# A macaron layer on one core: the scan's states, gates and squares get scheduling priority, and eight modulation sums move into the second feed-forward sublayer

## The chip, the cores and the metric

The kernel runs on one core of a Trainium2 chip. The metric is the device time of one execution in microseconds (us), as the median of several runs; less is better. A core has a matrix engine (PE, with the loading of its weights shown apart as PEld), a vector engine (DVE), a scalar engine (ACT), GpSimd (POOL) and an engine SP whose queue issues the transfers from memory (DMA). Each takes its instructions in a fixed order, and semaphores make one wait for another.

## What is computed

One layer on 512 tokens of width 1024: feed-forward 1, a mixer, feed-forward 2, each behind a norm whose shift, scale and gate come from a vector `c`, and a last norm. Cut from the reference:

```python
mod = silu(c) @ w_ada + b_ada        # 9 vectors of 1024: shift, scale, gate of 3 sublayers
x = x + 0.5 * gate0 * swiglu(modulate(rmsnorm(x), shift0, scale0), ffn1_in, ffn1_out)
x = x +       gate1 * hybrid_mixer(modulate(rmsnorm(x), shift1, scale1), ...)
x = x + 0.5 * gate2 * swiglu(modulate(rmsnorm(x), shift2, scale2), ffn2_in, ffn2_out)
x = rmsnorm(x, final_g)

def swiglu(h, w_in, w_out):
    a, b = jnp.split(h @ w_in, 2, axis=-1)
    return (jax.nn.silu(a) * b) @ w_out

def hybrid_mixer(h, ...):            # 24 heads of 64 in 4 groups
    u_pool, z, xbc, dt_raw = split(h @ w_in)
    y_pool = pool_mixer(u_pool, w_pool, pool_scale)   # windowed means, 4 windows
    xs, Bm, Cm = split(silu(causal_depthwise_conv(xbc)))
    y = ssd_chunked(xs, softplus(dt_raw), A, Bm, Cm) + d_skip * xs
    y = y * silu(z)
    y = y * lax.rsqrt(mean(y * y over the group) + EPS) * ssm_norm_g
    return concatenate([y_pool, y]) @ w_out
```

## The kernel before

**Matrix work.** Activations lie as 128 features by 512 tokens. Each fp32 product is made of three reduced-precision matmuls (L376 to L378) from a high and a low part of both sides. Weights come as raw blocks of 128x1024 (tile `w_raw`, three buffers); ACT casts the high part (L168), DVE subtracts to get the low part (L171), and both go into rings `w_hi` and `w_lo` of five. PE's order is written out by hand and fixed. The order on DVE, ACT, POOL and SP is made by a scheduler, which follows the program's order, dependences and priorities; `tc.high_priority()` raises the instructions inside it, and `keep_in_program_order` holds one to its place among others so marked.

**The mixer** goes through 46 tiles of products, n = 0 to 45: 33 of the in-projection (their order stands in a list), 8 called outA (n = 33 to 40) and 5 called outB. Tile n = 33 begins about 628 us into the execution. Between products the scan runs for 12 pairs of heads. Pair p has five steps at written times: `fetch`, `one` (transposes L1032, then exponentials L1037 on ACT and two products L1048 on DVE), `two` (PE states L1061 and diagonal part L1065, which reads L1048's result; then four states L1074 and the skip L1077 on DVE), `three` (PE L1087, which reads L1074's result; the gate: DVE L1088, POOL L473 and L1090) and `squares` (ACT L528, or L525 for a group's first pair, then POOL L473). Three pairs are a group: its squares are summed on PE (L494), a chain of ten small DVE operations takes the root (L507, L479, L481 to L488), PE spreads it over the partitions (L517), and DVE and ACT scale and split the group's outputs (L1108, L467, L469). The windowed means run on ACT, POOL and PE (L872 to L890), and outA adds to x by L603.

**Modulation sums.** Each of the 72 columns of `mod` is one DVE operation over 128x1024 (L549, with a read of the accumulator behind it), fed by a 512 KB transfer into a `w_raw` buffer (L559). A generator yields after each sum, `pump(n)` asks it for n, and it always loads one row ahead:

```python
for j, k in steps[len(ws):i + 2]:
    ws.append(self.W.block())
    self.nc.sync.dma_start(out=ws[-1], in_=self.a["ada"][j, k])
ins = self.ada_sum(*step, ws[i])
```

Before, the mixer makes the 32 sums of vectors 5, 7, 6 and 8: one at n = 1 to 8, at each even n from 10 to 32, one at each of the last four outA tiles, two in each outB tile. Vector 8 is the gate of feed-forward 2.

**Feed-forward 2.** After two halves of the norm come three plain pairs (`pair`, gated product L686), then 17 `quad`s that save matmuls by sums of halves. `combine` prepares these in four pumped steps of DVE and ACT work (L396, L400, L469). In a quad, DVE L440 adds PE's block y to `one`, and PE's block z, in the other half of y's bank, starts only when L440 has read y:

```python
block(y, ws[n:], [(act, HALF_A) for act in up], True)
V.tensor_tensor(out=one[:, la], in0=one[:, la], in1=y, op=ALU.add)   # L440
...
block(x, ws[n:], t2, False)
block(z, ws[:n], t1, True)
```

Feed-forward 1 is built alike, with sums of other vectors pumped between its quads.

Of the kernel before, what the change touches and what calls it, by code (L numbers as in the profile page):

```python
# [1 line left out]

# [1 line left out]

# [8 lines left out]
ALU = mybir.AluOpType  # L13
PSUM = bass.MemoryType.PSUM

P = 128
# [14 lines left out]
LATE2 = 2  # L31
MLATE = 5
SPREAD1, SPREAD2, SPREAD3 = 3.6, 1.8, 2.4
# [28 lines left out]
FULL = (0, NT)  # L62
# [220 lines left out]
class Block:  # L283
# [136 lines left out]
    def quad(self, h, g, outs):  # L420
# [39 lines left out]
        for src, c in ((two, lb), (x, la)):  # L460
            V.scalar_tensor_tensor(out=two[:, c], in0=src[:, c], scalar=-1.0, in1=one[:, c], op0=ALU.mult, op1=ALU.mult)
        self.split(two, *g)

    def split(self, src, hi, lo, sl=FULL, pool=False):
# [521 lines left out]
    @staticmethod  # L986
    def c_(c):
        return slice(c * P, (c + 1) * P)
# [64 lines left out]
    def two(self, p):  # L1053

        V, S, T, c_, v4 = self.nc.vector, self.nc.scalar, self.nc.tensor, self.c_, self.v4
        st = self.pair_st[p]
        heads, xd, xe, xs = st["heads"], st["xd"], st["xe"], st["xs"]
        btok = self.grp[p // 3]["btok"]
        pst = self.bank("t")
        for c in range(3):  # L1060
            T.matmul(pst[:, c_(c)], lhsT=btok[:, c_(c)], rhs=xe[:, c_(c)], start=True, stop=True)  # L1061
        yd = self.bank("y")
        for c in range(NCHK):
            for r in range(2):
                T.matmul(yd[64 * r:64 * (r + 1), c_(c)], lhsT=xd[:, c * P + 64 * r:c * P + 64 * (r + 1)],  # L1065
                         rhs=st["e"][r][:, c_(c)], start=True, stop=True)
        s = st["s"] = self.tmp()
        S.copy(out=s[:, c_(0)], in_=pst[:, c_(0)])
        ec = st["ec"]
        S.activation(out=ec[:, :3 * P], in_=ec[:, :3 * P], func=AF.Exp)  # L1070
        for c in (1, 2):
            for r in range(2):
                o = c * P + 64 * r
                V.scalar_tensor_tensor(out=s[:, o:o + 64], in0=s[:, o - P:o - P + 64],  # L1074
                                       scalar=self.dec[:, c, 2 * p + r:2 * p + r + 1], in1=pst[:, o:o + 64],
                                       op0=ALU.mult, op1=ALU.add)
        V.scalar_tensor_tensor(out=xs, in0=xs, scalar=self.vec[:, C_DS + p:C_DS + p + 1], in1=yd,  # L1077
                               op0=ALU.mult, op1=ALU.add)

    def three(self, p):  # L1080

        V, S, T, G, c_ = self.nc.vector, self.nc.scalar, self.nc.tensor, self.nc.gpsimd, self.c_
        st, gr = self.pair_st.pop(p), self.grp[p // 3]
        y, ec = st["xs"], st["ec"]
        yo = self.bank("y")
        for c in range(3):
            T.matmul(yo[:, c_(c)], lhsT=st["s"][:, c_(c)], rhs=gr["ct"][:, c_(c + 1)], start=True, stop=True)  # L1087
        V.tensor_tensor(out=ec[:, :3 * P], in0=ec[:, :3 * P], in1=yo[:, :3 * P], op=ALU.mult)  # L1088
        self.accumulate(y[:, P:], ec[:, :3 * P])
        G.tensor_tensor(out=y, in0=y, in1=self.z.pop(p), op=ALU.mult)  # L1090
        gr["y"].append(y)

    def squares(self, p):
        gr = self.grp[p // 3]
        if p % 3 == 0:
            gr["acc"] = self.big()
        self.square_into(gr["y"][p % 3], FULL, gr["acc"], p % 3 == 0)

    def group_sums(self, g):
        gr = self.grp[g]  # L1100
# [12 lines left out]
    def mixer(self, norm, after):  # L1113
        V = self.nc.vector
        self.z, self.convd, self.grp, self.pair_st = {}, {}, {}, {}
        acts = self.acts = {}
        h = norm.h
        order = self.mixer_order()
        self.cwh = self.vec[:, C_CW:C_CW + 100]
        self.sgh = self.vec[:, C_SG:C_SG + 12]  # L1120
        for t in (self.cwh, self.sgh):
            self.tc.keep_in_program_order(V.tensor_scalar(out=t, in0=t, scalar1=0.5, scalar2=None, op0=ALU.mult))

        def z_halves(pss, sl):
            for i, ps in enumerate(pss):
                self.silu_z(i, ps, sl)

        self.wdt = self.big()
        self.nc.sync.dma_start(out=self.wdt[:, :KD * 32], in_=self.a["w_dt"])
        self.in_halves(4, norm, z_halves)  # L1130
        self.bg = self.ada_steps((5, 7, 6, 8), True)
        plan = []

        def at(time, f, *args):
            plan.append((time, f, args))
            plan.sort(key=lambda e: e[0])

        def until(time):
            while plan and plan[0][0] <= time:
                _, f, args = plan.pop(0)  # L1140
                f(*args)

        for p, s in enumerate(STARTS):
            g = p // 3
            if p % 3 == 0:
                at(s + HEAD, self.head, g)
            for d, f in zip(STAGES, (self.fetch, self.one, self.two, self.three, self.squares)):
                at(s + d, f, p)
            if p % 3 == 2:
                at(s + SUMS, self.group_sums, g)  # L1150
                at(s + NORM, self.group_norm, g)

        self.wpool = None

        def pool(i, ps):
            if self.wpool is None:
                self.wpool = self.big()
                self.nc.sync.dma_start(out=self.wpool, in_=self.a["w_pool"])
            d = self.pool_mix(i, ps)

            def later():
                acts[i] = self.new_act()
                self.pool_out(i, d, acts[i])

            at(POOLS[i], later)

        def conv(i, ps):
            self.convd[i] = self.conv(i, ps)

        for n, (kind, i) in enumerate(order):  # L1170
            until(n)
            self.pump({"outA": i // 4, "outB": 2}.get(kind, 0 < n < 9 or n > 9 and n % 2 == 0))
            if kind in ("dt", "in"):
                ps = self.bank()
                if kind == "dt":
                    for part in range(2):
                        for k in range(KD):
                            o = 32 * (k % 4)
                            self.nc.tensor.matmul(ps[o:o + 32, :], lhsT=self.wdt[:, k * 32:(k + 1) * 32],
                                                  rhs=h[k][part].bitcast(F32), start=part == 0 and k < 4,  # L1180
                                                  stop=part == 1 and k >= 4)
                    dt = self.dt_all(ps)
                    for d in DT:
                        at(n + d, next, dt, None)
                    continue
                self.product(ps, None, h, mid=lambda f: until(n + f))
                if i < 4:
                    at(n + EVAC, pool, i, ps)
                elif i < 16:
                    at(n + EVAC, self.silu_z, i - 4, ps, FULL)  # L1190
                else:
                    at(n + EVAC, conv, i - 16, ps)
            else:
                ks = range(4, 10) if kind == "outA" else LAST_KS
                at(n + 1, self.out_full(i, [acts[k] for k in ks], 5, kind == "outB", lambda f: until(n + f)))
        until(len(order))
        assert not plan
        self.out_halves(range(MLATE, KD), [acts[k] for k in ks], 5, after(), SPREAD2)

    def run(self):  # L1200
        h, gs = self.start()
        norms = {}

        def norm(sub):
            norms[sub] = Norm(self, sub)
            return norms[sub]

        self.ffn(1, h, gs, 2, lambda: norm(1), LATE1, SPREAD1, (1, 1))
        self.mixer(norms[1], lambda: norm(2))
        gs = {j: self.new_act() for j in range(FIRST[2])}  # L1210

        def glu_halves(pss, sl):
            for i in range(2):
                self.glu(pss[2 * i], pss[2 * i + 1], sl, gs[i])

        self.in_halves(4, norms[2], glu_halves)
        final = Final(self, 0)
        self.bg = self.combine(norms[2].h)
        self.ffn(2, norms[2].h, gs, 8, lambda: final, LATE2, SPREAD3, (2, 0))
        final.finish()  # L1220


# [81 lines left out]
```

## Time and profile before

| | |
|---|---|
| median of 3 runs (lowest to highest) | 1098.95 us (1098.39 to 1099.58) |
| the profiled execution | 1098.18 us |
| its span, first to last instruction | 1096.3 us |
| granted TensorE clock, mean | 0.998 |
| PE / PEld busy | 1075.5 / 954.4 us |
| DVE / ACT / POOL busy | 851.2 / 500.6 / 116.9 us |

Busy time is the time in which an engine had an instruction running; the span is that of the profiled execution, with 1.9 us outside it. Matmuls overlap, so a busy PE is only one that had no gap. The feed-forwards and the mixer follow one another: feed-forward 2 is under way at 750 us and ends at the span's end.

### The profile page before, as it was taken

To read this page: it belongs to the slowest core of one execution; us is meant where nothing else is said; L and a number is where in the kernel's file an instruction comes from. 1 tells how busy PE (TensorE), PEld (TensorE's weight loads), DVE (VectorE), ACT (ScalarE), POOL (GpSimd) and SP (SyncE) were. 2 spreads that over 40 slices of the span, in tenths; PEclk is the share of its full clock that TensorE was granted. 3 is DMA by queue.
4 is the path that set the end of the run, shared out by engine and by line. 5 is a ranking of instruction groups with operands and counts; after the bars stand their busy time and mean duration, and the time that the engine had idled before them with its cause. 6 is when DMAs were issued, how large, how long until landed. Compare 5 with 4: busy or idle time off the path is not lost.

```text
span 1096.3 us, 17024 instructions
## 1 busy us (share of the span) xinstructions
PE 1075.5 (98%) x6764; PEld 954.4 (87%) x6764; DVE 851.2 (78%) x1354; ACT 500.6 (46%) x836; POOL 116.9 (11%) x114
## 2 busy tenths in 40 slices
PE   8999999999999999999999999999999999999997
PEld 7888899999899988887888767899899999999997
DVE  7986978888887848989988777764877778777744
ACT  4442444454444544656565552354434434444532
POOL 0000000000001410012312850121000000000011
PEclk9999999999999999999999999999999999999999
DMA  8865334443346405554445335740132233223222
GB/s 326 305 225 175 127 120 135 144 144 126 111 158 204 152 25 167 173 168 138 144 135 182 122 120 173 231 153 20 42 113 86 91 113 107 95 87 101 75 58 78
DMA packets 45955, 149.43 MB, mean 136 GB/s; under 512 B 5276, under 2 KB 8220, under 8 KB 45876
## 3 DMA queue, kind: packets, MB, share of 16 engines
q1 hardware_dynamic: 45876, 148.35, 41.8%
q8 instruction: 53, 0.87, 0.3%
q14 instruction: 26, 0.21, 0.1%
HBM read 146.18 MB, written 2.15 MB: 135 GB/s over the span
## 4 chain that ended last, share of the span: by engine, by line
PE 72%; DVE 14%; DMA 7%; ACT 4%; issue 2%; POOL 1%; SPq 0%; DVEq 0%; ACTq 0%; POOLq 0%
PE ps_mm L377 19%; PE ps_mm L376 19%; PE ps_mm L378 18%; PE ps_t L376 4%; PE ps_t L377 4%; PE ps_t L378 4%; DVE w_lo L171 3%; DVE w_raw L549 2%; DMA w_raw<-in_w_in_dram 2%; ACT w_hi L168 2%; DVE big L969 2%; DMA w_raw<-in_ada_dram 1%; DMA big<-csd 1%; ACT big L1035 1%; DVE big L973 1%
## 5 line engine op out<-in xcount | busy, mean ns | idle before, releaser
L376 PE MATMUL ps_mm<-big,w_hi 128*128 128x512 f32 (+1 forms) x1446 | 494.3, 342 | 0.5 <-DVE tmp L452 0.5
L377 PE MATMUL ps_mm<-big,w_hi 128*128 128x512 f32 (+1 forms) x1446 | 492.5, 341 | 0.4 <-DVE big L836 0.4
L378 PE MATMUL ps_mm<-big,w_lo 128*128 128x512 f32 (+1 forms) x1446 | 490.9, 339 | 0.0
L376 PEld LDWEIGHTS ps_mm<-big,w_hi 128*128 128x128 f32 x1446 | 272.1, 188 | 35.3 <-issue 2.3
L377 PEld LDWEIGHTS ps_mm<-big,w_hi 128*128 128x128 f32 x1446 | 274.0, 190 | 32.2 <-DVE big L836 0.9
L378 PEld LDWEIGHTS ps_mm<-big,w_lo 128*128 128x128 f32 x1446 | 271.6, 188 | 30.8
L168 ACT CAST w_hi<-w_raw 128x1024 fp32r<-128x1024 f32 (+1 forms) x118 | 120.2, 1019 | 250.2 <-issue 92.0
L171 DVE TENSOR_TENSOR w_lo<-w_raw,w_hi 128x1024 fp32r<-128x1024 f32 (+1 forms) x118 | 143.9, 1221 | 43.8 <-ACT w_hi L168 40.8
L168 ACT CAST w_hi<-row 128x1024 fp32r<-128x1024 f32 x124 | 116.6, 940 | 89.3 <-PE ps_t L377 37.9
L171 DVE TENSOR_TENSOR w_lo<-row,w_hi 128x1024 fp32r<-128x1024 f32 x124 | 134.9, 1088 | 22.4 <-ACT w_hi L168 22.4
L603 DVE SCALAR_TENSOR_TENSOR x<-ps_mm,mod,x 128x512 f32<-128x512 f32 (+1 forms) x111 | 74.7, 675 | 78.5 <-PE ps_mm L378 78.5
L376 PE MATMUL ps_t<-big,w_hi 128*128 128x256 f32 (+1 forms) x428 | 126.8, 296 | 1.9 <-DVE tmp L440 1.7
L377 PE MATMUL ps_t<-big,w_hi 128*128 128x256 f32 (+1 forms) x428 | 127.0, 297 | 0.0
L378 PE MATMUL ps_t<-big,w_lo 128*128 128x256 f32 (+1 forms) x428 | 126.6, 296 | 0.0
L473 POOL TENSOR_TENSOR sacc<-sacc,sq 128x256 f32<-128x256 f32 (+1 forms) x30 | 28.5, 951 | 754.2 <-ACT sq L528 443.5
L376 PEld LDWEIGHTS ps_t<-big,w_hi 128*128 128x128 f32 x428 | 80.5, 188 | 6.6 <-DVE tmp L440 3.0
L377 PEld LDWEIGHTS ps_t<-big,w_hi 128*128 128x128 f32 x428 | 81.5, 191 | 3.6
L378 PEld LDWEIGHTS ps_t<-big,w_lo 128*128 128x128 f32 x428 | 80.4, 188 | 2.1
L467 ACT CAST big<-tmp 128x512 fp32r<-128x512 f32 (+1 forms) x82 | 44.1, 546 | 21.5 <-DVE tmp L400 9.6
L469 DVE TENSOR_TENSOR big<-tmp,big 128x512 fp32r<-128x512 f32 (+1 forms) x66 | 41.5, 640 | 8.0 <-ACT big L467 7.6
L969 DVE SCALAR_TENSOR_TENSOR big<-ps_mm,vec,big 128x511 f32<-128x511 f32 (+2 forms) x60 | 44.6, 744 | 1.5 <-ACT big L967 0.8
L135 DVE TENSOR_TENSOR row<-row 128x1024 f32<-128x1024 f32 x31 | 37.9, 1222 | 3.7 <-DMA row<-in_ffn_inQ_dram 3.1
(180 smaller groups left out, 1149.1 us busy)
## 6 DMA issues: line engine op xcount, KB each, us to landing
w_raw<-in_ada_dram SPq DMA_DIRECT2D x56, 512.0 KB, 3.7
row<-in_ffn_inQ_dram SPq DMA_DIRECT2D x31, 768.0 KB, 4.4
w_raw<-in_ffn_out_dram SPq DMA_DIRECT2D x40, 512.0 KB, 3.8
w_raw<-in_w_in_dram SPq DMA_DIRECT2D x32, 512.0 KB, 3.7
row<-in_ada_dram SPq DMA_DIRECT2D x16, 512.0 KB, 6.4
row<-in_ffn_inQ_dram SPq DMA_DIRECT2D x31, 256.0 KB, 4.7
w_raw<-in_ffn_in_dram SPq DMA_DIRECT2D x14, 512.0 KB, 4.5
big<-csd SPq DMA_DIRECT2D x24, 256.0 KB, 4.3
```

What stands on the lines that cost most here:

```text
L135: V.tensor_tensor(out=raw[:, 1:4:2], in0=raw[:, 0:3:2], in1=raw[:, 3:4].broadcast_to([P, 2, NT]), op=ALU.add)
L168: nc.scalar.copy(out=h, in_=r)
L171: nc.vector.tensor_tensor(out=l, in0=r, in1=h.bitcast(F32), op=ALU.subtract)
L376: T.matmul(o, lhsT=hi, rhs=ahi[:, s], start=first, stop=False, skip_group_check=again)
L377: T.matmul(o, lhsT=hi, rhs=alo[:, s], start=False, stop=False, skip_group_check=again)
L378: T.matmul(o, lhsT=lo, rhs=ahi[:, s], start=False, stop=last, skip_group_check=again)
L467: self.nc.scalar.copy(out=hi[:, s], in_=src[:, :n])
L469: eng.tensor_tensor(out=lo[:, s], in0=src[:, :n], in1=hi[:, s].bitcast(F32), op=ALU.subtract)
L473: self.nc.gpsimd.tensor_tensor(out=acc, in0=acc, in1=q, op=ALU.add)
L549: return self.nc.vector.tensor_tensor_reduce(out=w, in0=w, in1=self.cb, scale=scale, scalar=bias, op0=ALU.mult, op1=ALU.add, accum_out=out)
L603: self.nc.vector.scalar_tensor_tensor(out=xs, in0=ps[:, :n], scalar=self.mod[:, gate, m:m + 1], in1=xs, op0=ALU.mult, op1=ALU.add)
L969: V.scalar_tensor_tensor(out=acc[:, s:], in0=ps[:, :NT - s], scalar=tap(3 - s), in1=acc[:, s:], op0=ALU.mult, op1=ALU.add)
```

## The change

Two things are done. The states L1074, the gate (L1088, L473, L1090) and the squares (L528 or L525, and their L473) are issued with high priority. And the eight sums of vector 8 leave the mixer: its pumps at n = 24 to 32 are dropped, outB gets one each instead of two, and feed-forward 2 makes the eight after `combine`, with three pumps behind each pair (two before) and two behind each quad (none before).

```diff
-        for c in (1, 2):
-            for r in range(2):
-                o = c * P + 64 * r
-                V.scalar_tensor_tensor(out=s[:, o:o + 64], ...
+        with self.tc.high_priority():
+            for c in (1, 2):
+                for r in range(2):
+                    o = c * P + 64 * r
+                    V.scalar_tensor_tensor(out=s[:, o:o + 64], ...
...
-        V.tensor_tensor(out=ec[:, :3 * P], in0=ec[:, :3 * P], in1=yo[:, :3 * P], op=ALU.mult)
-        self.accumulate(y[:, P:], ec[:, :3 * P])
-        G.tensor_tensor(out=y, in0=y, in1=self.z.pop(p), op=ALU.mult)
+        with self.tc.high_priority():
+            V.tensor_tensor(out=ec[:, :3 * P], in0=ec[:, :3 * P], in1=yo[:, :3 * P], op=ALU.mult)
+            self.accumulate(y[:, P:], ec[:, :3 * P])
+            G.tensor_tensor(out=y, in0=y, in1=self.z.pop(p), op=ALU.mult)
...
-        self.square_into(gr["y"][p % 3], FULL, gr["acc"], p % 3 == 0)
+        with self.tc.high_priority():
+            self.square_into(gr["y"][p % 3], FULL, gr["acc"], p % 3 == 0)
...
-        self.bg = self.ada_steps((5, 7, 6, 8), True)
+        self.bg = self.ada_steps((5, 7, 6), True)
...
-            self.pump({"outA": i // 4, "outB": 2}.get(kind, 0 < n < 9 or n > 9 and n % 2 == 0))
+            self.pump({"outA": i // 4, "outB": 1}.get(kind, 0 < n < 9 or 9 < n < 24 and n % 2 == 0))
...
-        self.bg = self.combine(norms[2].h)
-        self.ffn(2, norms[2].h, gs, 8, lambda: final, LATE2, SPREAD3, (2, 0))
+        self.pump(1000)
+        self.bg = chain(self.combine(norms[2].h), self.ada_steps((8,), True))
+        self.ffn(2, norms[2].h, gs, 8, lambda: final, LATE2, SPREAD3, (3, 2))
```

PE's 6117 instructions keep their order, row for row. Lines of the changed kernel are numbered one higher up to about L1070 (L549 becomes L550, L440 becomes L441), two to four higher behind it (L1074 becomes L1076, L1088 L1091, L1090 L1093, L1108 L1112). On POOL the order moves a little near the third group's last pair: the gate's L473 now stands behind three operations of a windowed mean that it stood ahead of, and the square's L473 ahead of one small copy that it stood behind.

DVE at the end of the scan, about n = 33 (`root` is the root of group 2, L1074 the states of pair 10, the first sum that of n = 32). Before:

```order
L488 SCALAR_TENSOR_TENSOR root<-root 128x4
L549 ISA w_raw,mod<-w_raw,cb,vec 128x1024
L549 ISA mod 128x1
L171 TENSOR_TENSOR w_lo<-w_raw,w_hi 128x1024 x2
L1108 SCALAR_TENSOR_TENSOR big<-big,vec,ps_mm 128x512 x3
L469 TENSOR_TENSOR big<-big 128x512
L1074 SCALAR_TENSOR_TENSOR tmp<-tmp,dec,ps_t 128x64
L469 TENSOR_TENSOR big<-big 128x512
L1074 SCALAR_TENSOR_TENSOR tmp<-tmp,dec,ps_t 128x64 x2
L469 TENSOR_TENSOR big<-big 128x512
L1074 SCALAR_TENSOR_TENSOR tmp<-tmp,dec,ps_t 128x64
L1077 SCALAR_TENSOR_TENSOR big<-big,vec,ps_y 128x512
```

Now:

```order
L489 SCALAR_TENSOR_TENSOR root<-root 128x4
L172 TENSOR_TENSOR w_lo<-w_raw,w_hi 128x1024 x2
L1076 SCALAR_TENSOR_TENSOR tmp<-tmp,dec,ps_t 128x64 x4
L1112 SCALAR_TENSOR_TENSOR big<-big,vec,ps_mm 128x512 x3
L470 TENSOR_TENSOR big<-big 128x512
L1079 SCALAR_TENSOR_TENSOR big<-big,vec,ps_y 128x512
```

The sum is gone from this place, and the four states stand together ahead of the group's scaling.

ACT somewhat later, at step `one` of pair 11 (L1035 and L1037 make its two exponentials, L528 is the square of pair 10, which reads what POOL's L1090 of that pair wrote). Before:

```order
L1035 ACTIVATE big<-big,cs 128x128 x5
L1037 ACTIVATE big<-big 128x512
L1035 ACTIVATE big<-big,cs 128x128 x3
L890 ACTIVATE tmp<-ps_t,vec 128x512
L1037 ACTIVATE big<-big 128x512
L467 CAST big<-tmp 128x512
L528 ACTIVATE sq<-big 128x512
```

Now:

```order
L1036 ACTIVATE big<-big,cs 128x128 x2
L529 ACTIVATE sq<-big 128x512
L1038 ACTIVATE big<-big 128x512
L1036 ACTIVATE big<-big,cs 128x128 x3
L891 ACTIVATE tmp<-ps_t,vec 128x512
L1038 ACTIVATE big<-big 128x512
L468 CAST big<-tmp 128x512
```

The square stands ahead of both exponentials of the next pair, where it stood behind them.

DVE in feed-forward 2, from the third pair's gated product to the first quad's add. Before:

```order
L686 TENSOR_TENSOR tmp<-tmp,ps_t 128x512
L469 TENSOR_TENSOR big<-big 128x256 x3
L469 TENSOR_TENSOR big<-tmp,big 128x512
L171 TENSOR_TENSOR w_lo<-row,w_hi 128x1024
L603 SCALAR_TENSOR_TENSOR x<-ps_mm,mod,x 128x512
L140 TENSOR_TENSOR row<-row 128x512
L603 SCALAR_TENSOR_TENSOR x<-ps_mm,mod,x 128x512
L171 TENSOR_TENSOR w_lo<-row,w_hi 128x512
L440 TENSOR_TENSOR tmp<-tmp,ps_t 128x256
```

Now, from the split of that product (ahead of these rows stand two more sums):

```order
L470 TENSOR_TENSOR big<-tmp,big 128x512
L550 ISA w_raw,mod<-w_raw,cb,hb 128x1024
L550 ISA mod 128x1
L604 SCALAR_TENSOR_TENSOR x<-ps_mm,mod,x 128x512 x2
L470 TENSOR_TENSOR big<-big 128x256
L550 ISA w_raw,mod<-w_raw,cb,hb 128x1024
L550 ISA mod 128x1
L470 TENSOR_TENSOR big<-big 128x256
L172 TENSOR_TENSOR w_lo<-row,w_hi 128x1024
L550 ISA w_raw,mod<-w_raw,cb,hb 128x1024
L550 ISA mod 128x1
L441 TENSOR_TENSOR tmp<-tmp,ps_t 128x256
```

Five sums thus stand ahead of the first quad's add, and L140 and the 128x512 L171 went behind it. Ahead of the second quad's add, directly behind the L469 that it followed, stand two more sums, and ahead of the third's the last one.

## Rows read from the trace of the kernel before

**Rows 1.** The profile's page, first part: busy us, share of the span, instructions.

```profile
PE 1075.5 (98%) x6764; PEld 954.4 (87%) x6764; DVE 851.2 (78%) x1354; ACT 500.6 (46%) x836; POOL 116.9 (11%) x114
```

**Rows 2.** Waits of PE: what waited, for what, total us, times, longest.

```profile
PE ps_mm L517 <- DVE root L488: 3.3, 3, 1.2
PE ps_mm L494 <- POOL big L473: 2.4, 1, 2.4
PE ps_t L376 <- DVE tmp L440: 1.7, 3, 1.0
PE ps_y L1087 <- DVE tmp L1074: 1.7, 2, 1.2
...
PE ps_y L1087 <- ACT tmp L890: 0.6, 1, 0.6
PE ps_y L1065 <- DVE big L1048: 0.5, 2, 0.3
```

**Rows 3.** Windows: length; busy us (instructions) of PE, PEld, DVE, ACT, POOL; clock, DMA.

```profile
600.00:625.00 25.00, 22.64 (x127) 18.65 (x126) 18.01 (x27) 14.91 (x34) 19.69 (x20) 1.00 0.52 170
625.00:650.00 25.00, 22.41 (x124) 16.90 (x124) 21.30 (x30) 13.22 (x29) 17.65 (x18) 1.00 0.29 93
...
750.00:775.00 25.00, 25.00 (x151) 22.22 (x150) 8.02 (x17) 7.40 (x15) 0.74 (x2) 1.00 0.07 22
775.00:800.00 25.00, 25.00 (x114) 20.48 (x114) 24.06 (x45) 11.72 (x21) 0.00 (x0) 1.00 0.14 43
```

**Rows 4.** Timelines of PE: start, us, instruction, [idle before <- releaser].

```profile
516.80 0.46 PE L517 MATMUL ps_mm<-vec,root 128*128 128x128 f32 x2 [0.98 <-DVE root L488]
...
628.07 0.94 PE L517 MATMUL ps_mm<-vec,root 128*128 128x128 f32 x7
...
669.10 0.57 PE L517 MATMUL ps_mm<-vec,root 128*128 128x128 f32 x3 [1.14 <-DVE root L488]
```

**Rows 5.** Timeline 604 to 622 of all engines, last gate and squares of group 2.

```profile
606.40 1.28 DVE L549 CUSTOM_DVE_ANT_0 w_raw<-w_raw,cb,vec 128x1024 f32<-128x1024 f32 x1
...
606.56 1.99 POOL L473 TENSOR_TENSOR big<-big,tmp 128x384 f32<-128x384 f32 x1 [4.44 <-DVE tmp L1088]
...
616.75 2.25 POOL L473 TENSOR_TENSOR big<-big,sq 128x512 f32<-128x512 f32 x1
...
619.06 1.05 PE L494 MATMUL ps_mm<-ones,big 128*128 128x1 f32 x8 [2.37 <-POOL big L473]
```

**Rows 6.** Timeline 622 to 650 of DVE.

```profile
625.79 1.00 DVE L488 SCALAR_TENSOR_TENSOR root<-root 128x4 f32<-128x4 f32 x1
626.71 2.12 DVE L549 CUSTOM_DVE_ANT_0 w_raw<-w_raw,cb,vec 128x1024 f32<-128x1024 f32 x1
```

**Rows 7.** Timeline 625 to 640 of POOL.

```profile
626.74 1.01 POOL L473 TENSOR_TENSOR big<-big,tmp 128x384 f32<-128x384 f32 x1
```

**Rows 8.** Timeline 634 to 648 of ACT.

```profile
646.91 0.63 ACT L528 ACTIVATE sq<-big 128x512 f32<-128x512 f32 x1 [0.37 <-POOL big L1090]
```

**Rows 9.** Timeline 282 to 287 of DVE, a quad of feed-forward 1.

```profile
283.58 1.28 DVE L549 CUSTOM_DVE_ANT_0 w_raw<-w_raw,cb,vec 128x1024 f32<-128x1024 f32 x1 [0.87 <-DMA w_raw<-in_ada_dram]
284.79 0.08 DVE L549 DVE_READ_ACCUMULATOR2_ANT mod<- 128x1 f32 x1
...
285.39 0.41 DVE L440 TENSOR_TENSOR tmp<-tmp,ps_t 128x256 f32<-128x256 f32 x1
```

**Rows 10.** Timeline 796 to 835 of DVE, the first quads of feed-forward 2.

```profile
797.54 0.68 DVE L140 TENSOR_TENSOR row<-row 128x512 f32<-128x512 f32 x1
...
799.08 0.75 DVE L603 SCALAR_TENSOR_TENSOR x<-ps_mm,mod,x 128x512 f32<-128x512 f32 x1 [0.85 <-PE ps_mm L378]
...
801.96 0.42 DVE L440 TENSOR_TENSOR tmp<-tmp,ps_t 128x256 f32<-128x256 f32 x1 [1.54 <-PE ps_t L378]
...
817.48 0.41 DVE L440 TENSOR_TENSOR tmp<-tmp,ps_t 128x256 f32<-128x256 f32 x1
```

**Rows 11.** Timeline 800 to 805 of PE, the start of the first quad's block z.

```profile
803.11 0.28 PE L376 MATMUL ps_t<-big,w_hi 128*128 128x256 f32 x1
```

More of the change, by code (lines that the diff above doesn't have):

```diff
@@ L1 @@
 from contextlib import ExitStack
+from itertools import chain
 import numpy as np
@@ L1070, in two @@
         S.activation(out=ec[:, :3 * P], in_=ec[:, :3 * P], func=AF.Exp)
-        for c in (1, 2):
-            for r in range(2):
-                o = c * P + 64 * r
-                V.scalar_tensor_tensor(out=s[:, o:o + 64], in0=s[:, o - P:o - P + 64],
-                                       scalar=self.dec[:, c, 2 * p + r:2 * p + r + 1], in1=pst[:, o:o + 64],
-                                       op0=ALU.mult, op1=ALU.add)
+        with self.tc.high_priority():
+            for c in (1, 2):
+                for r in range(2):
+                    o = c * P + 64 * r
+                    V.scalar_tensor_tensor(out=s[:, o:o + 64], in0=s[:, o - P:o - P + 64],
+                                           scalar=self.dec[:, c, 2 * p + r:2 * p + r + 1], in1=pst[:, o:o + 64],
+                                           op0=ALU.mult, op1=ALU.add)
         V.scalar_tensor_tensor(out=xs, in0=xs, scalar=self.vec[:, C_DS + p:C_DS + p + 1], in1=yd,
```

## The prediction

> **What bounds the kernel now.** I read the page's first part, then the list of PE's waits, then windows of 25 us, and then the timelines around each wait. PE is busy for 1075.5 of 1096.3 us [rows 1], its instructions and their order do not change, and no product is added or removed. So all that a change of the other engines' order can give or cost is PE's gaps. The list of waits shows what they are in the part that is edited [rows 2]: L517 waiting for the root chain, twice in the mixer, 0.98 and 1.14 us [rows 4] (the third is behind it); L494 waiting 2.4 us for POOL's square sum; L1087 waiting 1.7 us for the states L1074 and 0.6 us for ACT; L1065 waiting 0.5 us in two places. That is 7.3 us in the mixer, and the windows show where most of it lies: PE is busy 22.64 and 22.41 of 25 us between 600 and 650, and there POOL, busy for 116.9 us in all [rows 1], is busy 19.69 and 17.65 [rows 3]. A last wait in that list bears on the other half of the change: block z waiting for DVE's L440, 1.7 us in three places, all in feed-forward 1, where sums already run between quads.
>
> **What the priorities and the missing sums give in the mixer.** I take the waits in order of time.
>
> The root of group 0. Nine wide DVE operations stand in its chain before, six now, but a further 128x1024 weight split goes ahead of its first row. Three operations of 128x512 at 0.68 us (as L140, [rows 10]) less one of 128x1024, which I take to be as long as a sum, 1.21 us [rows 9], is 0.8 us; the wait is 0.98 [rows 4]. I take 0.8, bounds 0 and 1.0.
>
> L1065 near 575 us. One of its two waits (0.3 of 0.5 us, [rows 2]) stands behind a sum of the kind that is dropped. I take 0.3.
>
> L494 near 619 us. POOL is late by 2.37 us with the last square sum of group 2 [rows 5]. Its gate began at 606.56 with 1.99 us for the 128x384 L473, while the sum L549 of 606.40 ran on DVE; the same L473 takes 1.01 us at 626.74 [rows 7], where this time the sum, started 0.03 us ahead of it, takes 2.12 [rows 6] and not 1.28 as where POOL is idle [rows 9]. So when the two meet one of them pays 0.8 to 1.0 us. With the sum gone I give POOL that 1.0 us back, and the square sum now goes ahead of one small copy; the mean's three operations that have gone ahead of the gate's L473 take some of this again. The wait should be 0 to 1 us. But behind L494 the root chain is next: it ended at 626.79 [rows 6] for an L517 that PE began at 628.07 without a wait [rows 4]. It has 1.3 us to spare, and if PE comes 2.4 us earlier only part of that is kept. I take 1.5 us, bounds 0.5 and 2.4.
>
> The Trainium skill, "SBUF — State Buffer", section "SBUF: two separate sides", says that DVE and GpSimd share one pair of ports as an exclusive lock: a DVE operation with two inputs from SBUF and a GpSimd operation do not share it, the later one blocks for the whole of the other. The pairs of rows above agree in size (2.12 less 1.28 is 0.84, against 1.01 for POOL's operation), though here the one that started first by the trace was the one stretched. By that rule POOL's own work cannot be hurried by an order among its rows alone, and the gain at L494 comes only from the sums that leave; without the rule, taking 1.99 us as what that L473 costs, I would give L494 0.7 us less.
>
> L1087 near 638 us. DVE puts the four states among the scaling of group 2, and PE loses 1.7 + 0.6 us [rows 2]. Now they stand together ahead of the scaling: these 2.3 us go. What is late next is L1065 of pair 11. It reads DVE's L1048, that waits for ACT's second L1037, and on ACT the square of pair 10 now stands ahead of both. It can't start before POOL's L1090 of that pair is done; before, it waited for it until 646.91, 0.37 us [rows 8]. That is also about when PE then ran L1065. POOL's gate will be earlier, since DVE's L1088 goes ahead of pair 11's first operations, but PE too arrives 2.3 us earlier, and behind the square ACT has still to make both exponentials and DVE both L1048. I take a new wait of 1.3 us, near the low end as the gate is put forward; bounds 0 and 5, the 5 being the 2.3 us and four operations of 0.63 to 0.68 us, as L528 and L140 [rows 8, 10]. So a net gain of 1.0, bounds -2.7 and 2.3.
>
> The last root (669.10, [rows 4]). Its chain has a sum and a weight split in it before and after: nothing gained.
>
> The other gates, squares and states earn nothing: the list of waits [rows 2] has no PE wait on them, since products cover them. If that cover were gone, a gate would cost what it did at L494. The sums that leave also free transfers and buffers near the scan's end, which may bring the last outA weights earlier; that is in the bounds of the L1065 wait.
>
> Sum in the mixer: 0.8 + 0.3 + 1.5 + 1.0 = 3.6 us, with 0 to 6.5 as what the bounds leave likely.
>
> **What the eight sums cost in feed-forward 2.** One sum takes 1.28 us, 1.21 from its start to the row behind it [rows 9]. DVE has 8.02 of 25 us of work between 750 and 775, but 24.06 between 775 and 800 [rows 3], where `combine` runs; and the order puts all sums behind `combine`'s last step, five of them ahead of the first quad's L440. From there on it counts when L440 ends, for block z waits for it. Before, L440 ran from 801.96 to 802.38, and z began at 803.11 [rows 10, 11], 0.73 us later. I keep 0.08 for the hand-over: L440 may be 0.65 us late for nothing.
>
> First quad: five sums are 6.05 us; L140 (0.68 us, [rows 10]) and a split of the same 128x512 go behind L440, 1.3 us together; left are 4.75 us. DVE was idle for 0.85 and 1.54 us there [rows 10], both waits for PE, and they take 2.4; the 0.65 us takes the rest down to 1.75. Second quad: L440 (817.48, [rows 10]) directly follows an operation that it always followed, so two sums ahead of it are 2.42 us late, less 0.65, 1.8 us. Third: 1.21 less 0.65, 0.6 us. Feed-forward 1 shows that this is how it goes: there one sum ahead of an L440 that started at 285.39 [rows 9] cost PE the longest of the three waits, 1.0 us [rows 2]. The rows of `ada` come through the three `w_raw` buffers that the second weights use too, so the fifth may come late: up to 1 us more. Sum 4.1 us, bounds 2 (the order kept, but the waits half hidden) and 5.5.
>
> **Sum.** 4.1 - 3.6 = +0.5 us on the profiled execution's 1098.18, 1098.7; on the median, which is 0.8 above it, 1099.4. I say 1099.0, between the two. A measurement of this kernel can tell about 0.2%, 2.2 us, from no change.
>
> **Rivals.**
> *The sums are hidden.* DVE's idle time from 750 to 775 [rows 3] would take them if the early ones ran there, and then only the mixer's gain is left: 1098.95 - 3.6, about 1095.3. Against it stands the order: no sum ahead of `combine`'s last step. It needs a cost of 1.4 us or less.
> *The square holds up the exponentials.* If POOL's gate of pair 10 is not earlier, L1065 of pair 11 waits up to 5 us, the region near 640 loses 2.7 us in place of gaining 1.0, and the time is 1099.4 + 3.7, about 1103; with a wait of 3 us, 1101.1, which is the point where it decides. For it: the square was already waiting for that L1090 [rows 8]. The Trainium skill, "TensorE: Matmul & The Clock Gate", table at its head, has ScalarE's queue as strictly in order; the row with the square's wait agrees, and by it nothing behind the square can pass. Without such waiting the sum would be 1.3 us lower.
> *The priorities do not do what they say.* POOL stays as late for L494, 2.4 us, and the rest of the mixer gives 1 to 2: feed-forward 2's 4.1 us show as 1101 to 1102.
> *All of the mixer's 7.3 us go* and half the loss is hidden: about 1094.
>
> **Chances.** The forecast (1097 to 1101) 0.47; hidden sums 0.2 and the whole gain 0.06; the square 0.15; no effect of the priorities 0.12. Faster by over 0.2% 0.27, slower 0.25, the rest the same. The range takes in the middle of the cases on both sides: 1095.0 to 1102.2; the likeliest's own is 1097 to 1101.
>
> **What would show it.** In the list of waits after: L517 twice shorter or gone; L494's 2.4 us below 1; L1087 waiting for L1074 gone; L1065 waiting for L1048 up to 1 to 2 us; block z waiting for L440 up from 1.7 to near 6 us, with three new places at 803 to 840 us. POOL's L473 near 606 at about 1 us shows the meeting with the sum gone. I am wrong if block z does not wait there (then faster), or if the window from 625 to 650 has PE no busier than 22.4 us (then slower).

## The result, and the profile after

The changed kernel takes 1111.2 us (median of 4 runs, 1110.06 to 1112.01) against 1099.26 us for the kernel before (4 runs: the three known before, and one of 1101.9): a ratio of 1.0107, 95% interval 1.0091 to 1.0122. It is slower by 12 us, outside the range. The page of the profiled execution (1112.01 us) begins:

```profile
span 1110.2 us, 17028 instructions
...
PE 1083.3 (98%) x6764; PEld 959.5 (86%) x6764; DVE 849.4 (77%) x1354; ACT 500.9 (45%) x836; POOL 115.2 (10%) x114
```

DVE, ACT and POOL have as much work as before to within 2 us [rows 1]; PE's busy time is 8 us longer for the same 6764 matmuls. The list of PE's waits after (what waited, for what, total us, times, longest):

```profile
PE ps_t L377 <- DVE tmp L441: 7.0, 8, 2.6
PE ps_y L1066 <- DVE big L1049: 4.0, 3, 2.7
PE ps_t L1062 <- DVE tmp L1047: 3.3, 1, 3.3
...
PE ps_mm L518 <- DVE root L489: 0.8, 1, 0.8
...
PE ps_y L1089 <- DVE tmp L1076: 0.2, 1, 0.2
```

Read against [rows 2]: what was to go has gone. L495's wait for POOL (2.4 us as L494 before) is off the list, L1089's for the states is 0.2 of 1.7 us, and the mixer's two waits for the root, 0.98 and 1.14 us [rows 4], are gone, though group 2 has a new one of 0.8. (The third of the 3.3 us in [rows 2] is at 15 us, ahead of the mixer.) What has come is larger: L1062 and L1066 wait 3.3 and 4.0 us for DVE's products of steps `one`, and block z 7.0 us for the adds, 4.7 of them in feed-forward 2 where there were none. And the granted clock falls, which the windows show (length, busy us of PE, PEld, DVE, ACT, POOL, then the clock as a share of the full 2.4 GHz; 0.50 is the lower level, 1.2 GHz):

```profile
577.50:580.00 2.50, 0.30 (x2) 0.00 (x0) 1.60 (x3) 2.47 (x7) 0.00 (x0) 1.00 0.00 0
580.00:582.50 2.50, 1.44 (x10) 1.24 (x12) 2.12 (x4) 1.42 (x4) 0.00 (x0) 0.81 0.00 0
582.50:585.00 2.50, 2.50 (x18) 2.07 (x15) 1.65 (x6) 2.50 (x9) 0.00 (x0) 0.51 0.00 0
585.00:587.50 2.50, 2.50 (x12) 2.01 (x11) 2.50 (x3) 0.41 (x1) 0.00 (x0) 1.00 0.00 0
650.00:652.50 2.50, 0.14 (x2) 0.00 (x0) 1.57 (x1) 2.50 (x7) 2.18 (x2) 1.00 0.00 0
652.50:655.00 2.50, 1.36 (x12) 1.15 (x14) 2.44 (x8) 2.40 (x5) 0.00 (x0) 0.65 0.00 0
655.00:657.50 2.50, 2.50 (x12) 1.88 (x9) 1.96 (x3) 0.00 (x0) 0.00 (x0) 0.50 0.00 0
657.50:660.00 2.50, 2.50 (x8) 1.93 (x7) 0.43 (x1) 0.00 (x0) 0.00 (x0) 0.50 0.36 84
660.00:662.50 2.50, 2.50 (x14) 2.11 (x13) 0.76 (x1) 1.05 (x1) 0.00 (x0) 0.99 0.31 126
```

Each time PE stands nearly still (0.30 and 0.14 of 2.5 us), and then it works a while at half speed. That is one reason why its busy time has grown; the other is a lower clock at the start, of which more below.

Both traces have PE's 6764 matmuls in the same order, so the start of each can be taken from one trace and from the other, and the growth of the difference shows where the time went (times in brackets are those of the kernel before):

| stretch of the kernel before | growth, us |
|---|---|
| start and feed-forward 1, to 503 | +3.1 |
| root of group 0 (516) | -0.8 |
| pair 5, L1066 (533) | +0.7 |
| pair 7, L1062 (575): wait, then lower clock | +3.4, +0.9 |
| L495 (619), then pair 9 and the root of group 2 (622, 628) | -2.5, +1.3 |
| L1089 (638 to 641) | -2.8 |
| pair 11, L1066 (647): wait, then lower clock | +3.3, +2.7 |
| last root (669) | -1.2 |
| first three adds of feed-forward 2 (803, 819, 834) | +1.8, +2.7, +0.6 |

With small drifts between, the mixer is +5.3 us and feed-forward 2 +5.4 us. The 3.1 us ahead of the mixer are taken as no part of the change: the execution of before whose profile is shown has the clock at 1.00 between 10 and 20 us, where it was 0.66 to 0.83 in every other trace of this study, though the code there is the same. Executions of one kernel differ by as much (22 runs of before in one set went from 1096.71 to 1101.52 us). So single profiles are compared from the mixer on, and medians decide.

How the wait at pair 11 comes about stands in three timelines of the changed kernel, ACT, POOL and PE:

```profile
645.04 0.70 ACT L1036 ACTIVATE big<-big,cs 128x128 f32<-128x128 f32 x2
649.75 0.63 ACT L529 ACTIVATE sq<-big 128x512 f32<-128x512 f32 x1 [4.01 <-POOL big L1093]
650.29 0.61 ACT L1038 ACTIVATE big<-big 128x512 f32<-128x512 f32 x1
...
652.25 0.62 ACT L1038 ACTIVATE big<-big 128x512 f32<-128x512 f32 x1
```

```profile
646.76 1.39 POOL L474 TENSOR_TENSOR big<-big,tmp 128x384 f32<-128x384 f32 x1 [1.15 <-DVE tmp L1091]
648.23 1.48 POOL L1093 TENSOR_TENSOR big<-big 128x512 f32<-128x512 f32 x1
```

```profile
652.88 0.40 PE L1066 MATMUL ps_y<-big 128*64 128x128 f32 x2 [2.73 <-DVE big L1049]
654.04 1.97 PE L1066 MATMUL ps_y<-big 128*64 128x128 f32 x14 [0.77 <-DVE big L1049]
```

ACT had the input of its first exponential ready at 645.7 and then stood for 4.01 us, because the square of pair 10 was next in its order and POOL's gate of that pair ended at 649.7. Both exponentials, DVE's two L1049 and PE's L1066 came behind. Before, the square waited 0.37 us behind them [rows 8]. At pair 7 the square of pair 6 does a part of this:

```profile
575.34 0.63 ACT L526 ACTIVATE big<-big 128x512 f32<-128x512 f32 x1 [1.28 <-POOL big L1093]
...
577.05 0.62 ACT L1038 ACTIVATE big<-big 128x512 f32<-128x512 f32 x1
```

```profile
577.70 0.69 DVE L1049 TENSOR_TENSOR big<-big 128x512 f32<-128x512 f32 x1 [0.99 <-ACT big L1038]
...
580.36 0.55 DVE L1047 TENSOR_TENSOR tmp<-big,dst 128x384 f32<-128x384 f32 x1
```

The wait and the square take 1.8 us there, ACT's two L968 ahead of the exponential's input some more, and the exponential starts at 577.05. On DVE, L1047 makes the input of L1062. It stands behind the first L1049, and that one waited for the late exponential: L1047 ran at 580.36, and L1062 at 581.06. How much of this is the square's is for the experiments.

### The profile page after: what moved, and what is told of

Same layout as the page of the kernel before. It is cut to its first block, busy times and chain, and to the rows that moved or that the text cites. A ratio compares the mean times of both kernels' runs of the same rounds, so it can differ in the third digit from the quotient of the medians.

```text
span 1110.2 us, 17028 instructions
## 1 busy us (share of the span) xinstructions
PE 1083.3 (98%) x6764; PEld 959.5 (86%) x6764; DVE 849.4 (77%) x1354; ACT 500.9 (45%) x836; POOL 115.2 (10%) x114
## 4 chain that ended last, share of the span: by engine, by line
PE 70%; DVE 14%; DMA 6%; issue 4%; ACT 4%; POOL 1%; SPq 0%; DVEq 0%; ACTq 0%; POOLq 0%
PE ps_mm L377 18%; PE ps_mm L378 18%; PE ps_mm L379 18%; PE ps_t L377 4%; PE ps_t L378 4%; PE ps_t L379 4%; DVE w_lo L172 4%; DMA w_raw<-in_w_in_dram 3%; DMA w_raw<-in_ada_dram 2%; DVE w_raw L550 2%; DVE big L970 2%; ACT w_hi L169 1%; DVE big L470 1%; ACT big L1036 1%; PE ps_mm L495 1%
## 5 line engine op out<-in xcount | busy, mean ns | idle before, releaser
L474 POOL TENSOR_TENSOR sacc<-sacc,sq 128x256 f32<-128x256 f32 (+1 forms) x30 | 29.1, 969 | 761.4 <-ACT sq L529 445.3
L470 DVE TENSOR_TENSOR big<-tmp,big 128x512 fp32r<-128x512 f32 (+1 forms) x66 | 41.6, 639 | 7.8 <-ACT big L468 7.4
```

Of the source, the lines that this page charges most:

```text
L470: eng.tensor_tensor(out=lo[:, s], in0=src[:, :n], in1=hi[:, s].bitcast(F32), op=ALU.subtract)
L474: self.nc.gpsimd.tensor_tensor(out=acc, in0=acc, in1=q, op=ALU.add)
```

## The experiments

Each ratio is to the kernel before on the same chip, with its 95% interval.

**Priorities alone.** The sums are put back as they were:

```diff
-        self.bg = self.ada_steps((5, 7, 6), True)
+        self.bg = self.ada_steps((5, 7, 6, 8), True)
...
-        self.ffn(2, norms[2].h, gs, 8, lambda: final, LATE2, SPREAD3, (3, 2))
+        self.ffn(2, norms[2].h, gs, 8, lambda: final, LATE2, SPREAD3, (2, 0))
```

> The changed kernel with the eight sums back in the mixer: priorities on states, gates and squares only. Theory A (the square stands ahead of the next pair's exponentials on ACT, waits there for POOL, and PE's states and diagonal parts come late, after which the granted clock falls): the two places of the changed kernel, pairs 7 and 11, wait again, 3 us each with a piece at the lower clock behind it; feed-forward 2 as before. Time about 1104, 5 us above the kernel before. Theory B (the sums that left the mixer changed buffers and transfers, and that made the waits): no such waits, 1095 to 1099.

1109.15 us, ratio 1.0091 (1.0076 to 1.0106): slower than either theory's number. Both waits are there and longer, and behind each the lower clock is back. The list of waits has

```profile
PE ps_t L1062 <- DVE tmp L1047: 5.9, 2, 4.5
PE ps_y L1066 <- DVE big L1049: 4.4, 3, 3.3
```

In the mixer this profile loses 8.8 us against before, 3.5 more than with the sums moved. So B falls, and the priorities by themselves make most of the loss. But L494's wait for POOL and L1087's for the states are off the list here too, with every sum where it was: in the starts 2.3 and 2.8 us are gained at these two places, as in the changed kernel.

**The sums moved alone.** The kernel before with the change's other half: the eight sums in feed-forward 2, nothing raised.

> The kernel before with only the eight sums moved into feed-forward 2, no priorities. Theory A: the mixer loses its wait at 575 us at most and keeps the others, so it is within 1 us of before; feed-forward 2 loses 5.2 us at the adds of its first three quads (1.8, 2.7 and 0.6 as in the changed kernel). Time about 1104. Theory B: mixer 5 us worse, time about 1109.

1103.08 us, ratio 1.0028 (1.0015 to 1.0042). Feed-forward 2 loses as A says: 1.7, 2.6 and 0.6 us at the three adds in its profile, one of its fastest executions (1099.8). But the mixer, which A had within 1 us of before, gains 4.7 us. By these stretches the kernel would be 0.5 us above before; the median is 3.6 above, and the 3 us between are in no trace that was kept. The windows of this profile from 600 to 650, where [rows 3] have PE busy for 22.64 and 22.41:

```profile
600.00:625.00 25.00, 24.70 (x134) 20.24 (x133) 14.11 (x20) 14.35 (x33) 18.29 (x22) 1.00 0.40 125
625.00:650.00 25.00, 23.49 (x134) 18.15 (x133) 23.88 (x39) 14.49 (x30) 17.75 (x16) 1.00 0.29 93
```

The waits for POOL's square and for the states are gone with no priority at all. On DVE the states of pair 10 still stand among the scaling, as before, but all of it runs 5 to 6 us earlier. First the kernel before, then this one:

```profile
633.89 2.15 DVE L171 TENSOR_TENSOR w_lo<-w_raw,w_hi 128x1024 fp32r<-128x1024 f32 x1 [3.09 <-ACT w_hi L168]
635.97 2.05 DVE L1108 SCALAR_TENSOR_TENSOR big<-big,vec,ps_mm 128x512 f32<-128x512 f32 x3
...
640.33 0.27 DVE L1074 SCALAR_TENSOR_TENSOR tmp<-tmp,dec,ps_t 128x64 f32<-128x64 f32 x1
```

```profile
627.14 3.16 DVE L172 TENSOR_TENSOR w_lo<-w_raw,w_hi 128x1024 fp32r<-128x1024 f32 x2
630.23 2.05 DVE L1109 SCALAR_TENSOR_TENSOR big<-big,vec,ps_mm 128x512 f32<-128x512 f32 x3
...
635.15 0.27 DVE L1075 SCALAR_TENSOR_TENSOR tmp<-tmp,dec,ps_t 128x64 f32<-128x64 f32 x1
```

Before, the second of the two weight splits waited for a block whose transfer went out at 628.87, just as the sum of 626.71 had ended and given a `w_raw` buffer back; here both splits follow the root at once. So it was the sum, with its buffer, that held up the scaling. The states are late by it only as long as they stand in the scaling: with the priorities alone the second split still waits 3.05 us, but the states are ahead of the scaling, and PE's L1087 of that pair does not wait for them.

**The squares without priority.** The changed kernel with one line taken back:

```diff
-        with self.tc.high_priority():
-            self.square_into(gr["y"][p % 3], FULL, gr["acc"], p % 3 == 0)
+        self.square_into(gr["y"][p % 3], FULL, gr["acc"], p % 3 == 0)
```

> The changed kernel with the priority taken from the squares alone; states, gates and the move stay. Theory A: on ACT the square of pair 10 stands behind both exponentials of pair 11 again and that of pair 6 behind the first of pair 7, so the waits of 3 us and the low clock behind them go; the mixer is 2 to 4 us shorter than before, feed-forward 2 5.2 us longer: 1100 to 1102. Theory C (the gates and states themselves delay the exponentials' products): the waits at pairs 7 and 11 stay and the time is near 1110.

1102.08 us, ratio 1.0017 (0.9999 to 1.0035): 9 us less than the changed kernel, from this line alone. L1062 is off the list of waits, L1066 is at 1.5 us of 4.0, and the mixer gains 4.9 us against before, which is what the moved sums alone gave it. So A stands at both pairs, C falls, and the priority on states and gates is worth nothing beside the moved sums. In this profile the clock fell in feed-forward 2 instead, behind the second quad's add: 0.71 and 0.61 between 820 and 825 us, 1.6 us lost there. That was behind a wait of 1.95 us; in the changed kernel's profile a longer one at that add, 2.55 us, was not followed by a fall. Why one is and another not stays open.

**The sums behind the add.** In the changed kernel, with `in_quad` 2 in feed-forward 2 and 0 in feed-forward 1:

```diff
         V.tensor_tensor(out=one[:, la], in0=one[:, la], in1=y, op=ALU.add)
+        self.pump(self.in_quad)
...
-        self.ffn(2, norms[2].h, gs, 8, lambda: final, LATE2, SPREAD3, (3, 2))
+        self.ffn(2, norms[2].h, gs, 8, lambda: final, LATE2, SPREAD3, (2, 0))
```

> The changed kernel, but in feed-forward 2 the sums are issued inside the quads directly behind the add that releases block z: two sums stand ahead of the first quad's add (five in the change), none ahead of the second's and third's. If the sums ahead of the add are what feed-forward 2 lost, its waits for that add fall from 5.2 us to under 0.5, and the time is 5 us below the changed kernel, about 1106. If the transfers or DVE's total work are what it lost, it stays near 1111.

1107.92 us, ratio 1.0078 (1.0063 to 1.0093): 3.3 us less, not 5. The waits for the add are down to what feed-forward 1 has, but feed-forward 2 still loses 2.2 us. A new wait of 1.1 us in all shows what is late next: block x of the next quad waits for an ACT copy. DVE's weight splits now come behind the sums; that this is what makes the copy late is read from the order and was not tested:

```profile
PE ps_t L377 <- DVE tmp L441: 1.5, 4, 0.7
PE ps_mm L377 <- ACT tmp L439: 1.1, 2, 0.6
```

**No priorities, sums behind the add.** The kernel with the sums moved alone, and these sums behind the add as in the last run.

> No priorities; the eight sums in feed-forward 2 directly behind the adds that release block z (two ahead of the first quad's add, then two behind each add). The mixer should keep the gain of the sums moved alone (4.7 us in its profile), and feed-forward 2 should lose the 2.2 us that it lost with the sums behind the add, not 5.1: about 1097, 2 to 3 us below the kernel before. If the two places are not independent, or the sums cost their DVE time wherever they stand, 1100 or more.

1098.11 us, ratio 0.9989 (0.9979 to 0.9999), 0.9 us below before. The mixer's gain is kept (4.9 us in the profile), feed-forward 2 loses 2.1 us; the profile's sum is 2.8 us, the medians show less.

**No priorities, sums early.** Against the kernel with the sums moved alone:

```diff
-        self.bg = chain(self.combine(norms[2].h), self.ada_steps((8,), True))
-        self.ffn(2, norms[2].h, gs, 8, lambda: final, LATE2, SPREAD3, (3, 2))
+        self.bg = self.ada_steps((8,), True)
+        self.pump(1000)
+        self.bg = self.combine(norms[2].h)
+        self.ffn(2, norms[2].h, gs, 8, lambda: final, LATE2, SPREAD3, (2, 0))
```

> No priorities; the eight sums issued between the norm's halves and the first pair of feed-forward 2, ahead of the preparation of the quads, where DVE was busy for 8 of 25 us. If DVE's idle time hides them, feed-forward 2 loses under 1 us and the time is about 1095.5, 4 us below the kernel before. If the rows' transfers or the later preparation hold up the first quad, it loses 2 to 5 us, and the time is 1097 to 1100.

1095.67 us, ratio 0.9971 (0.9957 to 0.9985), 3.4 us below before: the lowest median of all. The mixer gains 4.6 us, feed-forward 2 loses 1.7, all of it at the first quad's add. The sums stand in DVE's idle time, some waiting for their rows:

```profile
757.75 1.28 DVE L550 CUSTOM_DVE_ANT_0 w_raw<-w_raw,cb,hb 128x1024 f32<-128x1024 f32 x1
...
761.59 1.29 DVE L550 CUSTOM_DVE_ANT_0 w_raw<-w_raw,cb,hb 128x1024 f32<-128x1024 f32 x1 [1.34 <-DMA w_raw<-in_ada_dram]
...
770.39 1.28 DVE L550 CUSTOM_DVE_ANT_0 w_raw<-w_raw,cb,hb 128x1024 f32<-128x1024 f32 x1 [0.99 <-DMA w_raw<-in_ada_dram]
```

**The waits filled.** In the changed kernel, 12 products of 128x512 for each of the pairs 7 and 11 (for pair 7 ahead of L1062, for pair 11, shown, ahead of L1066):

```diff
+        for _ in range(12 if p == 11 else 0):
+            T.matmul(yd, lhsT=fill[:, :P], rhs=fill, start=True, stop=True)
```

> The changed kernel, with 12 further products of 128x512 on PE (2.8 us) where it waits at step two of pairs 7 and 11; their result is overwritten. If the lower granted clock behind the two waits comes from PE standing still there, the clock stays at its upper level, the waits vanish into the products, and the 1 and 2.7 us behind them are saved: about 3 to 4 us below the changed kernel, 1107.5. If the lower clock has another cause, the time is that of the changed kernel or above, 1111 to 1113.

1107.97 us, ratio 1.0079 (1.0062 to 1.0097): 3.2 us below the changed kernel, although PE has 5.5 us of useless work more. The squares are where they were and the delay up to the scan's products is the same (3.3 and 2.8 us in the difference of starts), but the clock stays up:

```profile
577.50:580.00 2.50, 2.05 (x13) 1.43 (x13) 2.22 (x4) 1.75 (x4) 0.00 (x0) 1.00 0.00 0
580.00:582.50 2.50, 2.50 (x23) 2.06 (x22) 2.50 (x7) 1.15 (x3) 0.00 (x0) 1.00 0.04 13
...
650.00:652.50 2.50, 1.68 (x18) 1.04 (x16) 2.48 (x8) 2.39 (x5) 0.00 (x0) 1.00 0.00 0
652.50:655.00 2.50, 2.50 (x12) 1.98 (x11) 2.29 (x3) 0.00 (x0) 0.00 (x0) 1.00 0.00 0
```

So it was PE's standing still that brought the lower clock. Behind the two waits the difference of starts grew by 0.9 and 2.7 us in the changed kernel; here it changes by -0.6 and 0.0. The price of the lower clock was thus about 1.5 and 2.7 us by the profiles; the medians show 3.2 for both, and their intervals (1.0091 to 1.0122, and this one) just overlap.

**Squares alone.** The kernel before with only the squares' priority.

> The kernel before with priority on the squares alone, all sums where they were. On ACT the squares of pairs 6 and 10 stand between the two exponentials of pairs 7 and 11, and that of pair 7 ahead of both of pair 8. Theory A: new waits of PE for the states' or diagonal products' inputs at pairs 7, 8 and 11, of 1 to 4 us, with the clock falling behind the longer: 1102 to 1106. If a square ahead of the exponentials does no harm by itself, the time is that of before within 1 us.

1104.05 us, ratio 1.0041 (1.0025 to 1.0057): the time is as A says, the way is not. The square of pair 7 does stand ahead of both exponentials of pair 8 and waits 1.34 us for POOL, but PE does not wait for it; the order of the other instructions gave it room. The loss is at the root of group 0, which PE waits for 2.5 us, and at pair 10's L1087 and what follows (2.7 us), where the clock falls too (0.70 and 0.62 between 645 and 650 us). L494 waits 2.5 us for POOL as before: the squares' priority by itself did not even free the wait that it is nearest to.

```profile
PE ps_mm L494 <- POOL big L473: 2.5, 1, 2.5
PE ps_mm L517 <- DVE root L488: 2.5, 1, 2.5
```

**Sums split.** Four early, two ahead of the first quad's add, two behind it, no priorities.

> No priorities; four of the eight sums between the norm's halves and the first pair of feed-forward 2, two ahead of the first quad's add and two directly behind it. The first quad's add had 1.6 us of wait with all eight early; if that came from the quads' preparation being pushed back by eight sums, it falls under 1 us here and the time is that of the early sums or 0.5 us below, about 1095. If two sums ahead of the first add cost as they did before, it is 1096 to 1098.

1097.77 us, ratio 0.9990 (0.9980 to 1.0000). Feed-forward 2 lost 0.6 us in the profile (the mixer gained 3.4), as it would if the preparation pushed back by eight sums was what the first quad paid for; yet the median is not better than with all sums early. Inconclusive: medians of one set of runs and another differ by about as much.

**States and gates with sums early.** The priority on states and gates kept, none on squares.

> The kernel with the eight sums early, and the priority on states and gates (not squares) kept. If these priorities earn nothing beside the moved sums, it is within 1 us of the early sums alone, 1095 to 1096.5. If states and gates ahead help at the scan's end, 1 to 2 us less; if they hold up what they pass, 1 to 3 us more.

1097.66 us, ratio 0.9987 (0.9977 to 0.9997). The interval overlaps that of the early sums without priorities (0.9957 to 0.9985); by the medians these priorities cost up to 2 us, by the profiles (the mixer gains 4.6 us in both) nothing. They do not help. Nor is it shown which of the four kernels below before is the best (no priorities with the sums behind the add, early or split, and this one): from the mixer on their profiles are all 2.6 to 3.0 us below before, while their medians are 0.9, 3.4, 0.6 and 0.7 below.

## Why the prediction was wrong

**The mixer: +5.3 us where 3.6 us were to be gained.** The terms of the sum came out near their sizes (forecast in brackets): the root of group 0 gave 0.8 (0.8), L494 with what followed 1.2 (1.5), L1087 2.8 (2.3), and the last root 1.2 (nothing). What failed were two steps on what the raised squares would cost, and a term that the sum did not have.

The first is "The other gates, squares and states earn nothing [...] since products cover them", which put pair 7 at nothing. That looked only at PE's waits before, and so at what a priority could gain. It did not ask what each raised instruction passes. The rows of the order for pair 11 were read for this, and the same order stood at pair 7, which was not looked at: it cost 3.4 us, and the clock behind it. The prediction's own words on pair 11, "on ACT the square of pair 10 now stands ahead of both", describe the cause at both. With the squares alone put back, both waits went and the kernel was 9 us faster. The Trainium skill, "TensorE: Matmul & The Clock Gate", table at its head, has ACT's queue as strictly in order; the 4.01 us for which ACT stood agree.

The second is the size at pair 11: "a new wait of 1.3 us, near the low end as the gate is put forward". It was 3.3 us. The gate was put forward on DVE (L1091 ahead of L1045), but PE too had come 2.8 us earlier through the wait at L1087 that went: POOL's L1093 ended at 649.7, only 0.4 us ahead of where PE began to wait, and the square, both exponentials and both L1049 were still to come. The rival of the square named the mechanism and 5 us as its bound; it was given 0.15 and should have been the forecast. Even its 1103 left out pair 7 and the clock. The sign set for a slower kernel, PE no busier than 22.4 us between 625 and 650, did not show this either (24.02): pair 11's wait had moved behind 650.

**What a wait costs was taken as the wait.** Nothing in the sum stood for the clock. The trace of before has a wait of 2.37 us with no fall behind it [rows 5], and so showed no price; behind the waits of 3.3 and 2.7 us the starts lost 0.9 and 2.7 us more, and the filled waits show the clock to be theirs.

**Feed-forward 2: 5.1 us at the adds for 4.1.** First quad 1.8 (1.75) and third 0.6 (0.6) as worked out. The second was 2.7 for 1.8: L470 ahead of the sums was itself 0.9 us late against PE, behind a wait of 1.95 us for the row of weights of the next quad, whose transfer had gone out late:

```profile
822.26 1.23 DVE L136 TENSOR_TENSOR row<-row 128x1024 f32<-128x1024 f32 x1 [1.95 <-DMA row<-in_ffn_inQ_dram]
```

```profile
815.27 0.33 SPq L123 DMA_DIRECT2D row<-in_ffn_inQ_dram  x1
```

It went out as the 128x512 split ended (815.25) that the change had put behind the first quad's add, 2 us after block z of that quad began; before, it went out at 800.46, 2.7 us ahead of that block. The prediction counted this split as about 0.7 us gained at the first quad, and did not ask what waits for its end.

The rival that the sums would be hidden was wrong for this order. Put early, in the idle time that it named, they cost 1.7 us, near the 1.4 that it allowed.

**To whom the gain belonged.** The prediction gave the priorities the gain at L1087 and part of that at L494. Both gains are there with either half of the change: 2.8 and 2.5 us with the sums moved alone, 2.8 and 2.3 with the priorities alone and the sums in place. So they do not add, and states and gates raised beside the moved sums change nothing. (At L494 the priorities' part is not clean: PE comes there 6 us later, through the wait at pair 7, and the other engines have had that time too.) Beside the moved sums the raised squares make all that the priorities lose; no run has the squares taken back with the sums in place, so the 8.8 us that the priorities lose alone are not split.

**L494: the size was right, the way was not.** The prediction let the gate's L473 fall from 1.99 to about 1 us as the sum left, and had the gain come only from sums that leave. In the changed kernel that operation (now L474) still takes 1.99 us, beside a weight split of DVE (615.44, 1.94 us); with the priorities alone and the sum still there it takes 0.99:

```profile
616.26 1.99 POOL L474 TENSOR_TENSOR big<-big,tmp 128x384 f32<-128x384 f32 x1
```

```profile
615.54 1.60 DVE L550 CUSTOM_DVE_ANT_0 w_raw<-w_raw,cb,vec 128x1024 f32<-128x1024 f32 x1
...
619.14 0.99 POOL L474 TENSOR_TENSOR big<-big,tmp 128x384 f32<-128x384 f32 x1
```

L494's wait went in both. What is shorter in both is POOL's work behind that operation: the gate's second product 1.27 us (2.25 before) and the square's sum 1.29 (2.25). That can't be all, for with the squares alone raised they take 1.28 and 1.71 and the wait stays. So 1.2 us for 1.5 was luck in part: what brings the sum of squares forward stays open, and no run took the sum and the gate apart at 606 us alone.

Two slips of reading changed little: the third wait for the root, put behind the mixer, is at 15 us; and the upper bounds of the mixer's terms add to 6.0 us, not 6.5.

What is not settled: 12 us by the medians are 5.3 + 5.4 by the profile from the mixer on; the other 1 us is within what executions differ by. Which waits bring the lower clock is open: 1.95, 2.7 and 3.3 us did, 2.37 and 2.55 did not.

## What to carry to other kernels

A priority is a change to everything it passes: before raising an instruction that waits for another engine, list what stands behind it on its own engine and who waits for that, at every place where the loop issues it and not only at the one to be mended. A raised instruction whose input is late turns its engine's queue into the wait, so look first whether taking work or a buffer's user away from the place makes room without any priority. Background work belongs in an engine's idle stretch, not in front of the operation that frees a bank.

## What the runs showed of the hardware that was not expected

Behind a wait in which PE had worked 0.14 of 2.5 us, the granted clock was at its lower level, 0.50, for nearly 7 us (653 to 660) and cost 2.7 us, as much as the wait itself; with useless products in that wait and one more it stayed at 1.00, and the kernel was 3.2 us faster by the medians for 24 products more. Filling a wait that can't be removed can thus pay.
